# Rearranging the first part, the SSD steps and the output weights of a Hymba-style encoder step on one Trainium2 core

## The chip, the core and the metric

The kernel runs on one core of a Trainium2 chip. The metric is the device time of one execution in microseconds (us), as the median of several runs. Five engines work side by side and each takes its instructions strictly in its program's order: TensorE (PE in the profile, with PEld for its weight loads), VectorE (DVE), ScalarE (ACT), GpSimd (POOL) and SyncE (SP). DMAs are issued here from the instruction queues of SP and ACT, so an issue that must wait holds up whatever stands behind it on that engine.

## The reference

One layer of a streaming encoder is computed for 2048 prompt tokens and for 8 streams of 16 sample tokens; together they are 17 tiles of 128 tokens.

```
n = rmsnorm(x, norm1_g)
z, xbc, dt_raw, q, k, v, f_raw = split_columns(n @ w_in)
y_ssd = ssd_mixer(z, conv(xbc), dt_raw, ...)      # 8 heads, state 128, gate, group norm
y_fox = attention(q, k, v) with forget gates       # 8 heads of 64, causal
h = x + concat(y_ssd, y_fox) @ w_out
x = h + (silu(conv(n2 @ w_up)_g) * conv(n2 @ w_up)_v) @ w_down,   n2 = rmsnorm(h, norm2_g)
y = rmsnorm(x, final_norm_g)
```

The keys, values, forget logs, SSD states and convolution rows are outputs too. A matrix product with a weight matrix is made of three products of high and low parts ("hi" and "lo"): `split` rounds an fp32 tile to `hi` and subtracts to get `lo`.

## The kernel before

**Stages.** The prompt is cut into four parts of 512 tokens (two windows of 256 each; part 0 also carries the sample tile). `a_head(p)` makes the normalized, transposed input `nT` of a part: `sizes` finds each token's row size, a diagonal matrix `dg` of it is multiplied with ones into a PSUM tile (L203), and `rows` scales the transposed x with it (L208), then splits the product into hi (ACT, L102) and lo (POOL for the first half of the rows of a window, DVE for the second, L105). `a_body(p)` multiplies `nT` with the columns of `w_in`, 256 or 272 columns at a time with tokens as output rows (`proj_tm`, L366 to L368) or 128 columns at a time as output rows (`proj_cm`, L413 to L415). Each weight tile is loaded (`craw`) and split by ACT and POOL into `cmw`.

**Attention** runs over 4 x 8 (part, head) pairs and 320 units. A unit is one step of `t_phase`: a 128x512 score tile (L692, L693), its exponential on ACT (L697), and, two units behind, the product with the values (L662). One step of `s_phase` for the next head goes with it: a score tile (L634) whose maximum DVE takes (L637). `end` normalizes two heads: four reciprocals (L680) and a product.

**Filling.** TensorE's order is written out by hand in the loop at the end of the function. `fill` says how many credits of projection work (`part_steps`, later `out_steps`) go into a unit, and `sides` how many steps of `sample_attention` or of `ssd_chunk` are spread over a part's units. Before unit 0 the loop runs eight score steps with 1.5 credits of projection each. The word `"wait"` lets four units pass without filling. The other engines' orders come from a scheduler that looks at this order.

**SSD.** `ssd_chunk(c)` handles one tile of 128 tokens: loads, the decay matrix `sg` (a DMA broadcast, a subtraction on POOL L499, a minimum on DVE L500, an exponential on ACT L501), transposes, products, gate and norm. The sample tile `SMP` has eight inner steps, one for each stream: it loads that stream's state into `s0`, a buffer of the tag `yl` (two buffers, which attention uses too), multiplies (L555, L559), updates it on DVE (L561, L562) and stores it.

**Output.** When the projections are done, the pools of stage A are closed and `out_weights` loads and splits all eight tiles of `w_out` in one go (L853, L102, L105); three "wait" words follow, then `out_proj` runs as filling. After attention come the last output tiles and the feed-forward part (`ffn_part`), which fills the second half of the time.

**Tags.** A tile's tag names a ring of buffers: `cmw` 3, `xt` 2, `k12` 4 (attention's keys), `yl` 2, `sg` 1, `raw` 2. The profile's names drop the numbers, so `k12` is `k` and `q12` is `q`.

## Time and profile before

| what | us |
|---|---|
| median of 3 runs | 3183.7 (3178.56 to 3184.08) |
| the profiled execution's own time | 3180.02 |
| its span, first to last instruction | 3178.3 |
| TensorE busy | 3035.1 (95%) |
| VectorE busy | 1829.3 (58%) |
| ScalarE busy | 1024.1 (32%) |
| GpSimd busy | 882.4 (28%) |
| mean granted TensorE clock | 0.978 |

Busy time of an engine is the union of its instructions. PEclk is the share of full clock that TensorE was granted; a matmul at 0.50 takes twice its time and counts as busy. A row of a timeline has start, duration, engine, line, operation and tiles, and in brackets how long the engine had been idle and who ended that. A row of waits has the total, the number of waits and the longest. A row of grouped instructions has the count, then busy time and the mean in ns, then the idle time of the engine ahead of them and who ended it. An engine's name with a q is its instruction queue, which issues a DMA.

### The profile page before, as it was taken

To read this page: it belongs to the slowest core of one execution; us is meant where nothing else is said; L and a number is where in the kernel's file an instruction comes from. 1 tells how busy PE (TensorE), PEld (TensorE's weight loads), DVE (VectorE), ACT (ScalarE), POOL (GpSimd) and SP (SyncE) were. 2 spreads that over 40 slices of the span, in tenths; PEclk is the share of its full clock that TensorE was granted. 3 is DMA by queue.
4 is the path that set the end of the run, shared out by engine and by line. 5 is a ranking of instruction groups with operands and counts; after the bars stand their busy time and mean duration, and the time that the engine had idled before them with its cause. 6 is when DMAs were issued, how large, how long until landed. Compare 5 with 4: busy or idle time off the path is not lost.

```text
span 3178.3 us, 45508 instructions
## 1 busy us (share of the span) xinstructions
PE 3035.1 (95%) x17808; PEld 2671.8 (84%) x17808; DVE 1829.3 (58%) x3325; ACT 1024.1 (32%) x1778; POOL 882.4 (28%) x574
## 2 busy tenths in 40 slices
PE   5998988899999998999999999999999999999999
PEld 5886866788778875677899999989999999999998
DVE  5355465757574655552355555566555556766666
ACT  3343332434333433322322222233222223322222
POOL 3223311332232223100232232323232232433332
PEclk9998988999999998999999999999999999999999
DMA  4856864576547545543621221233122222322221
GB/s 161 256 180 197 246 200 128 165 215 178 148 152 211 157 137 178 169 144 111 234 79 58 64 67 54 67 100 100 53 74 60 67 66 71 109 74 80 68 71 67
DMA packets 233854, 398.36 MB, mean 125 GB/s; under 512 B 62624, under 2 KB 118568, under 8 KB 233640
## 3 DMA queue, kind: packets, MB, share of 16 engines
q1 hardware_dynamic: 180072, 234.22, 23.9%
q10 hardware_dynamic: 53568, 161.24, 16.2%
q8 instruction: 140, 2.29, 0.3%
q14 instruction: 74, 0.61, 0.1%
HBM read 317.13 MB, written 78.25 MB: 124 GB/s over the span
## 4 chain that ended last, share of the span: by engine, by line
PE 84%; DMA 7%; DVE 4%; issue 2%; SPq 1%; POOL 1%; ACT 1%; ACTq 0%; POOLq 0%; DVEq 0%
PE mm L113 11%; PE mm L114 11%; PE mm L115 11%; PE pv L662 6%; PE dn L975 5%; PE dn L976 5%; PE dn L977 5%; PE mm L413 3%; PE mm L414 3%; PE mm L415 3%; PE dn L873 2%; PE mm L366 2%; PE dn L875 2%; PE mm L367 2%; PE dn L874 2%; PE mm L368 2%
## 5 line engine op out<-in xcount | busy, mean ns | idle before, releaser
L105 POOL TENSOR_TENSOR wr<-raw,wr 128x1024 fp32r<-128x1024 f32 x198 | 475.9, 2411 | 1032.8 <-ACT wr L102 985.8
L113 PE MATMUL mm<-nT,wr 128*128 128x386 f32 (+1 forms) x2112 | 696.5, 330 | 1.3 <-ACT wr L102 0.8
L114 PE MATMUL mm<-nT,wr 128*128 128x386 f32 (+1 forms) x2112 | 695.3, 329 | 0.1
L115 PE MATMUL mm<-nT,wr 128*128 128x386 f32 (+1 forms) x2112 | 694.5, 329 | 0.0
L953 DVE SCALAR_TENSOR_TENSOR ac<-mm,cw,ac 128x384 f32<-128x384 f32 (+1 forms) x528 | 301.7, 572 | 345.0 <-ACT ac L951 337.3
L951 ACT ACTIVATE ac<-mm,cw 128x384 f32<-128x384 f32 (+1 forms) x264 | 172.5, 653 | 785.9 <-PE mm L115 782.0
L978 DVE TENSOR_TENSOR y<-y,dn 128x512 f32<-128x512 f32 x374 | 255.3, 684 | 267.3 <-PE dn L977 264.5
L114 PEld LDWEIGHTS mm<-nT,wr 128*128 128x128 f32 x2112 | 399.4, 189 | 6.8 <-DVE nT L105 0.3
L113 PEld LDWEIGHTS mm<-nT,wr 128*128 128x128 f32 x2112 | 397.6, 188 | 7.7 <-ACT wr L102 1.1
L115 PEld LDWEIGHTS mm<-nT,wr 128*128 128x128 f32 x2112 | 398.0, 188 | 5.7
L105 POOL TENSOR_TENSOR cmw<-craw,cmw 128x1024 fp32r<-128x1024 f32 (+1 forms) x96 | 231.1, 2411 | 380.4 <-ACT cmw L102 295.9
L413 PE MATMUL mm<-nT,cmw 128*128 128x256 f32 (+2 forms) x1024 | 309.2, 302 | 1.6 <-DVE g_2k L300 1.6
L637 DVE TENSOR_REDUCE nm<-s 128x1 f32<-128x512 f32 (+2 forms) x320 | 192.5, 606 | 190.2 <-PE s L634 109.4
L414 PE MATMUL mm<-nT,cmw 128*128 128x256 f32 (+2 forms) x1024 | 298.6, 292 | 0.0
L415 PE MATMUL mm<-nT,cmw 128*128 128x256 f32 (+2 forms) x1024 | 297.9, 291 | 0.0
L662 PE MATMUL pv<-pr,v 128*128 128x512 f32 (+3 forms) x640 | 295.6, 552 | 2.2 <-POOL v L602 1.8
L975 PE MATMUL dn<-wr,ht 128*128 128x512 f32 x748 | 294.4, 394 | 2.8 <-DVE y L978 1.7
L976 PE MATMUL dn<-wr,ht 128*128 128x512 f32 x748 | 292.8, 391 | 0.0
L977 PE MATMUL dn<-wr,ht 128*128 128x512 f32 x748 | 290.1, 391 | 0.0
L102 ACT CAST wr<-raw 128x1024 fp32r<-128x1024 f32 x198 | 203.2, 1042 | 173.7 <-PE dn L977 161.5
L697 ACT ACTIVATE pr<-s 128x512 f32<-128x512 f32 (+1 forms) x320 | 169.7, 531 | 269.7 <-PE s L693 182.9
L634 PE MATMUL s<-ks,q 68*128 68x512 f32 (+2 forms) x320 | 201.4, 635 | 10.8 <-DMA q<-q_d 7.0
(287 smaller groups left out, 5194.9 us busy)
## 6 DMA issues: line engine op xcount, KB each, us to landing
raw<-in_w_up ACTq DMA_DIRECT2D x132, 512.0 KB
raw<-in_w_down ACTq DMA_DIRECT2D x66, 512.0 KB
craw<-in_w_cm ACTq DMA_DIRECT2D x64, 512.0 KB
k<-k_d SPq DMA_DIRECT2D x80, 256.0 KB
craw<-in_w_tm ACTq DMA_DIRECT2D x24, 512.0 KB
q_d<-qk SPq DMA_DIRECT2D x96, 128.0 KB
k_d<-qk SPq DMA_DIRECT2D x96, 128.0 KB
ks<-k_d SPq DMA_DIRECT2D x80, 136.0 KB
```

The costliest lines, as they stand in the source:

```text
L105: leng.tensor_sub(lo, src, hi.bitcast(F32))
L113: T.matmul(ps[:, :W], whi(k), wt[:, 0, k, :W], start=k == 0, stop=False)
L114: T.matmul(ps[:, :W], whi(k), wt[:, 1, k, :W], start=False, stop=False)
L115: T.matmul(ps[:, :W], wlo(k), wt[:, 0, k, :W], start=False, stop=k == n - 1)
L413: T.matmul(ps[:, :W], wc[:, 0, k, :], wk[:, 0], start=k == 0, stop=False)
L414: T.matmul(ps[:, :W], wc[:, 0, k, :], wk[:, 1], start=False, stop=False)
L415: T.matmul(ps[:, :W], wc[:, 1, k, :], wk[:, 0], start=False, stop=k == KT - 1)
L662: m = T.matmul(pv[:, of:512], vr[:, jj], pr[:, :512 - of], start=first, stop=last)
L953: V.scalar_tensor_tensor(ac[:, 0:n], ps[:, j:j + n], cw2[:, ct, j:j + 1], ac[:, 0:n], op0=ALU.mult, op1=ALU.add)
L975: T.matmul(ps, ht[:, 0, ts_], wd[:, 0, cc], start=x == 0, stop=False)
L976: T.matmul(ps, ht[:, 0, ts_], wd[:, 1, cc], start=False, stop=False)
L977: T.matmul(ps, ht[:, 1, ts_], wd[:, 0, cc], start=False, stop=x == len(g) - 1)
```

## The change

**Part 0's head.** The row sizes no longer come from a second copy of x. `sizes_by_columns` squares the transposed tiles that are loaded anyway (ACT), and sums them by 8 matmuls with a column of ones per token tile (40 in all, L186 of the changed file). The diagonal is made on ACT instead of DVE (`diagonals`). The transposed x has its own tag `xT` of two buffers. The first window is prepared ahead of the first projection; the second and the sample tile are prepared between the first four half tiles of it. The twelve DMAs of constant rows (L1110 in the old file) are now issued at step 12 of the body.

**Heads of parts 1 to 3** are cut into more steps (sizes at step 12, diagonals at step 40, each window's rows in two halves), with waits of 1, 3 and 1 units instead of one of 4. `xt` has one buffer instead of two.

**SSD.** Two more steps for each chunk; chunk 3 moves from part 1 to part 2, and the counts in `sides` are set to the real number of steps. The subtraction and the minimum become eight `Relu` activations, one for each head, and the exponential takes the sign. `s0` takes its buffer from `k12`.

**Attention.** The four reciprocals and the closing product of `end` are queued as `chores`, one for each following unit. The eight first steps get 3.0 credits each.

**Weights.** `split2` makes lo on POOL in two halves; `proj_tm`, `proj_cm` and `out_weights` use it. `out_weights` loads two tiles ahead (on SP's queue instead of ACT's), splits one tile at a time behind the latest exponential, and waits 3 units first and 2 after each tile, so 19 units in place of 12.

```diff
+    def split2(src, hi, lo, leng):
+        S.copy(hi, src)
+        m = src.shape[1] // 2
+        for c in (slice(0, m), slice(m, 2 * m)):
+            leng.tensor_sub(lo[:, c], src[:, c], hi[:, c].bitcast(F32))
...
+        def sizes_by_columns(n, xTs):
+            sq = at([P, 2, 4, 256], "cmw", WA)
+            for kk in range(2):
+                S.activation(sq[:, kk, :, :n * P], xTs[kk][:, :, :n * P], AF.Square)
+            pz = tpt()
+            for c in range(n):
+                for k in range(KT):
+                    T.matmul(pz[:, c:c + 1], sq[:, k // 4, k % 4, c * P:(c + 1) * P], ones[:, 0:1], start=k == 0, stop=k == KT - 1)
+            ss = at([P, 2], "ss", 4)
+            V.tensor_scalar(ss[:, 0:n], pz[:, 0:n], 1.0 / D, EPS, op0=ALU.mult, op1=ALU.add)
+            G.tensor_tensor(ss[:, 0:n], ss[:, 0:n], mhalf[:, 0:n], op=ALU.pow)
...
-                dg = at([P, P], "dg", 4)
-                V.tensor_scalar_mul(dg, ident, ss)
+                dg = at([P, P], "dg", 2)
+                S.activation(dg, ident, AF.Identity, scale=x)
...
-        G.tensor_sub(sg, sg, acs[:, c].unsqueeze(2).to_broadcast([P, 8, P]))
-        V.tensor_scalar_min(sg, sg, 0.0)
-        S.activation(sg, sg, AF.Exp)
+        for h in range(8):
+            S.activation(sg[:, h], sg[:, h], AF.Relu, scale=-1.0, bias=acs[:, c, h:h + 1])
+        S.activation(sg, sg, AF.Exp, scale=-1.0)
...
-                s0 = bt_([P, 512], "yl", 2)
+                s0 = bt_([P, 512], "k12", KB)
...
-                    V.reciprocal(dn[:, cc], dn[:, cc])
+                    chores.append(lambda cc=slice(a * P, (a + 1) * P): V.reciprocal(dn[:, cc], dn[:, cc]))
+                chores.append(norm)
...
+        load(0)
+        load(1)
+        yield ("wait", 3)
         for k in range(KT):
-            raw = op.tile([P, D], F32, tag="raw", name="raw", bufs=2)
-            dW(raw, i["w_out"][0, k * P:(k + 1) * P, :])
             w = op.tile([P, 2, D], F32R, tag="wo", name="wo", bufs=KT)
-            split(raw, w[:, 0], w[:, 1], S, G)
+            with tc.issue_after(exps[-1]):
+                split2(raws[k], w[:, 0], w[:, 1], G)
             wo.append(w)
+            if k + 2 < KT:
+                load(k + 2)
+            yield ("wait", 2)
...
-    sides = {0: (sample_attention, 5 * NB + 1), 1: (lambda: chunks(SMP, 0, 1, 2, 3), 66), 2: (lambda: chunks(4, 5, 6, 7), 40),
-             3: (lambda: chunks(*range(8, 16)), 80)}
+    sides = {0: (sample_attention, 5 * NB + 1), 1: (lambda: chunks(SMP, 0, 1, 2), 49), 2: (lambda: chunks(3, 4, 5, 6, 7), 51),
+             3: (lambda: chunks(*range(8, 16)), 81)}
...
-                credit += 1.5
+                credit += 3.0
```

**What it moves.** First, ScalarE at the program's start. In the kernel before, five loads of x in its first layout (`in_xr`) stand ahead of the weights (`craw`), and the squares are of these:

```order
L98 DMA g1c<-in_g1c 128x8
L169 DMA cmw<-in_xr 128x1024 x5
L356 DMA craw<-in_w_tm 128x1088
L174 ACT_TABLE_LOAD
L174 ACTIVATE cmw,ss<-cmw 128x1024
L356 DMA craw<-in_w_tm 128x1088
L174 ACTIVATE cmw,ss<-cmw 128x1024 x3
```

In the kernel after, `xT` and `qk` are the transposed x of the first and second window:

```order
L98 DMA g1c<-in_g1c 128x8
L387 DMA craw<-in_w_tm 128x1088 x2
L182 ACT_TABLE_LOAD
L182 ACTIVATE cmw<-xT 128x1024 x2
L109 CAST cmw<-craw 128x1088 x2
L1123 ACTIVATE abc<-abc 128x8
L387 DMA craw<-in_w_tm 128x4x256
L182 ACTIVATE cmw<-qk 128x1024 x2
L387 DMA craw<-in_w_tm 128x4x256
L206 ACTIVATE dg<-ident,ss 128x128 x2
L102 CAST nT_134<-xT 128x4x256 x2
```

The `xr` loads are gone, and the diagonals and casts of the first window now stand behind the weights' casts and behind the squares of the second window.

Second, the decay matrix of an SSD chunk in part 2. In the kernel before, VectorE has the minimum (L500) among its maxima (L637):

```order
L533 TENSOR_TENSOR yt_8376<-yt_8376,s_8443 128x512
L467 SCALAR_TENSOR_TENSOR cth_8426<-cth_8426,cac_8425 128x256
L637 TENSOR_REDUCE nm_8333<-s_8488 128x1
L500 TENSOR_SCALAR sg_8813<-sg_8813 128x1024
L458 SCALAR_TENSOR_TENSOR cac_8503<-mm_8460,cw1_219,cac_8503 128x256
L637 TENSOR_REDUCE nm_8333<-s_8521 128x1
```

In the kernel after, ScalarE has the whole chain among its exponentials (`pr`) and evictions (`ev`):

```order
L733 ACTIVATE pr_9151<-s_9148 128x512
L419 ACTIVATE ev_9187<-mm_9135 128x256
L733 ACTIVATE pr_9195<-s_9192 128x512
L532 ACTIVATE sg_9396<-sg_9396,acs_185 128x128 x8
L533 ACTIVATE sg_9396<-sg_9396 128x1024
L109 CAST cmw_9469<-craw_9467 128x1088
L733 ACTIVATE pr_9233<-s_9230 128x512
```

The instruction that waits for the DMA of `sg` has moved from GpSimd to ScalarE, and nothing of the chain is left on VectorE.

Third, GpSimd at the output weights (`wo`). In the kernel before, with the memory fills of the value tiles (`v`) and the decay chain between them:

```order
L105 TENSOR_TENSOR wo_12535<-raw_12533,wo_12535 128x1024
L499 TENSOR_TENSOR sg_12763<-sg_12763,acs_235 128x1024
L105 TENSOR_TENSOR wo_12540<-raw_12538,wo_12540 128x1024
L602 MEMSET v_12855 128x4x64
L105 TENSOR_TENSOR wo_12545<-raw_12543,wo_12545 128x1024
L105 TENSOR_TENSOR wo_12550<-raw_12548,wo_12550 128x1024
L108 TENSOR_SCALAR ss_12736<-ss_12736 128x2
```

In the kernel after:

```order
L636 MEMSET v_12976 128x4x64
L112 TENSOR_TENSOR wo_12878<-raw_12734,wo_12878 128x512 x2
L557 TENSOR_TENSOR xe_12867<-xd_12863,te_186 128x512
L636 MEMSET v_13056 128x4x64
L112 TENSOR_TENSOR wo_12938<-raw_12826,wo_12938 128x512 x2
L636 MEMSET v_13143 128x4x64
L112 TENSOR_TENSOR wo_13001<-raw_12882,wo_13001 128x512 x2
```

Each pair of halves now has a fill or an SSD step between it and the next. Counted on TensorE's order by its L692 (L728 in the changed file), the units without any projection work ahead of the output products are 222 to 235 before and 224 to 251 after; around the head of part 1 they are 11 to 14 before and 9 to 15 after, around that of part 2 they are 51 to 54 before and 52 to 58 after.

More of the change, by code (lines that the diff above doesn't have):

```diff
@@ new lines, in a_head, with load @@
+                todo.append((e, w, SMP, 1, PAD1 + w[1] - w[0], i["xTs"]))
+        def load(e, w, c0, n, col, xsrc):
+            xTs = []
+            for kk in range(0, KT, 4):
+                xT = at([P, 4, 256], "qk" if first and e and n == 2 else "xT", 2)
+                dma(xT[:, :, :n * P], xsrc[:, kk:kk + 4])
+                xTs.append(xT)
+            return xTs
+        def sizes_by_columns(n, xTs):
[9 more added lines that the diff above has]
+            G.tensor_tensor(ss[:, 0:n], ss[:, 0:n], mhalf[:, 0:n], op=ALU.pow)
+            return [ss[:, c:c + 1] for c in range(n)]
@@ new lines, in sizes, with diagonals @@
+        def sizes(c):
+            ss = at([P, 2], "ss", 4)
+            for hf in range(2):
+                xt = at([P, 512], "xt", XB)
+                dA(xt, i["xr"][c][:, hf * 512:(hf + 1) * 512])
+                S.activation(xt, xt, AF.Square, accum_out=ss[:, hf:hf + 1])
+            V.tensor_add(ss[:, 0:1], ss[:, 0:1], ss[:, 1:2])
+            rsq(ss[:, 0:1], D)
+            return ss[:, 0:1]
+        def diagonals(ss):
+            dgs = []
+            for x in ss:
+                dg = at([P, P], "dg", 2)
+                S.activation(dg, ident, AF.Identity, scale=x)
@@ L211, in rows @@
                       V if kk else G)
-        ds = []
+                if not kk:
+                    yield
         if first:
             for t in todo:
-                rows(*t, sizes(*t))
-            yield 0.0
-            return
-        for t in todo:
-            ds.append(sizes(*t))
-        yield 0.0
-        for t, d in zip(todo, ds):
-            rows(*t, d)
-            yield 0.0
+                xTs = load(*t)
+                dgs = diagonals(sizes_by_columns(t[3], xTs))
+                yield
+                for _ in rows(*t, xTs, dgs):
+                    pass
+                yield
+            return
+        xTs = load(*todo[0])
+        ss = [sizes(todo[0][2] + c) for c in range(4)]
+        yield
+        dgs = diagonals(ss[0:2])
+        yield
+        yield from rows(*todo[0], xTs, dgs)
+        xTs = load(*todo[1])
+        dgs = diagonals(ss[2:4])
+        yield
+        yield from rows(*todo[1], xTs, dgs)
+        yield
     def gates(p, dtf):
@@ L357, in proj_tm @@
                 we = at([P, 2, 4, 272], "cmw", WA, F32R)
-                split(raw[:, :, :n], we[:, 0, :, :n], we[:, 1, :, :n], S, G)
+                split2(raw[:, :, :n], we[:, 0, :, :n], we[:, 1, :, :n], G)
                 wm.append(we)
@@ L402, in load_cm @@
             wc = at([P, 2, KT, P], "cmw", WA, F32R)
-            split(raw[:, 0:D].rearrange("p (k c) -> p k c", c=P), wc[:, 0], wc[:, 1], S, G)
+            split2(raw[:, 0:D].rearrange("p (k c) -> p k c", c=P), wc[:, 0], wc[:, 1], G)
             return wc
@@ L657, in hybrid_step @@
     pv_ins = []
-    late = []
+    late, chores, exps = [], [], []
     def weigh(pv, vr, jj, of, pr, first, last, end):
@@ L710, in t_rest @@
             weigh(a[0], *x)
+        while chores:
+            chores.pop(0)()
     def attention():
@@ L1035, in ffn_part @@
             finish(c)
-    for _ in a_head(0):
-        pass
+    head0 = a_head(0)
+    next(head0)
+    next(head0)
     tri = cb.tile([P, P], F32, name="tri")
@@ L1127, in part_steps @@
                 break
-            if k == 12 and hd:
+            if k in (12, 40) and hd:
                 next(hd)
@@ L1133, in part_steps @@
         next(hd)
-        yield "wait"
+        yield ("wait", 1)
         next(hd)
-        for c in hd:
-            pass
+        yield ("wait", 3)
+        next(hd)
+        yield ("wait", 1)
+        next(hd)
         bodies.append(a_body(p + 1))
@@ L1148, in out_steps @@
         open_out()
-        psum["wo"] = out_weights()
-        yield "wait"
-        yield "wait"
-        yield "wait"
+        yield from out_weights()
         for c in [SMP] + list(range(11)):
```

77 lines of the change are left out of this document (33 added, 44 removed).

## The prediction

> **What bounds the kernel now.** I read the page first, then the busy times in stretches, then the waits of TensorE. The page says that TensorE is the bound and that its clock is not always full:
>
> ```profile
> PE 3035.1 (95%) x17808; PEld 2671.8 (84%) x17808; DVE 1829.3 (58%) x3325; ACT 1024.1 (32%) x1778; POOL 882.4 (28%) x574
> PEclk9998988999999998999999999999999999999999
> ```
>
> So only what makes TensorE idle or slow can be gained. I cut the span at the places where the clock or the busy share falls (stretch, its length, then busy us and count for PE, PEld, DVE, ACT and POOL, then clock, DMA share and GB/s):
>
> ```profile
> 0.00:39.00 39.00, 3.51 (x9) 2.34 (x10) 24.04 (x59) 13.83 (x19) 18.08 (x31) 1.00 0.57 200
> 39.00:144.00 105.00, 103.00 (x734) 101.33 (x734) 37.23 (x106) 30.01 (x69) 31.79 (x14) 1.00 0.67 200
> 144.00:163.00 19.00, 14.20 (x70) 10.72 (x69) 12.22 (x42) 7.40 (x17) 4.62 (x7) 0.73 0.84 289
> 163.00:255.00 92.00, 88.11 (x689) 80.84 (x688) 49.66 (x144) 35.25 (x74) 24.07 (x16) 0.98 0.57 179
> 255.00:306.00 51.00, 40.27 (x304) 31.32 (x303) 29.23 (x72) 23.36 (x50) 17.03 (x15) 0.77 0.56 190
> 306.00:450.00 144.00, 136.93 (x1165) 118.13 (x1165) 77.98 (x198) 52.58 (x115) 39.96 (x22) 0.98 0.80 237
> 450.00:478.00 28.00, 18.51 (x125) 15.19 (x124) 17.09 (x30) 7.48 (x15) 5.24 (x3) 0.76 0.51 150
> 478.00:550.00 72.00, 57.05 (x302) 48.13 (x301) 35.94 (x71) 15.50 (x31) 12.47 (x9) 0.86 0.42 131
> 550.00:600.00 50.00, 42.41 (x275) 34.49 (x274) 37.39 (x69) 20.81 (x41) 16.67 (x15) 0.90 0.51 163
> 600.00:1190.00 590.00, 573.97 (x3826) 468.58 (x3825) 362.35 (x678) 234.35 (x464) 162.79 (x127) 0.99 0.58 170
> 1190.00:1240.00 50.00, 34.92 (x99) 21.43 (x99) 26.19 (x31) 18.70 (x29) 21.93 (x14) 0.69 0.64 195
> 1240.00:1577.00 337.00, 333.96 (x1567) 248.43 (x1565) 155.84 (x243) 98.08 (x189) 32.52 (x55) 1.00 0.49 161
> 1577.00:3178.00 1601.00, 1588.29 (x8666) 1490.89 (x8666) 964.14 (x1587) 466.80 (x668) 495.23 (x250) 1.00 0.24 73
> ```
>
> What a stretch loses is its length less (PE busy times clock). In order that gives 35.5, 2.0, 8.6, 5.7, 20.0, 9.8, 13.9, 22.9, 11.8, 21.8, 25.9, 3.0 and 12.7 us, together 193.6. The change doesn't touch the last two stretches; 178 us can be fought for, and no more.
>
> A short wait costs twice, as one place shows (a score tile that had waited, and the 4 us behind it):
>
> ```profile
> 697.95 0.47 PE L692 MATMUL s<-q,k 128*128 128x512 f32 x1 [2.12 <-DVE xd L565]
> 698.00:702.00 4.00, 4.00 (x12) 2.54 (x13) 2.96 (x6) 2.63 (x8) 0.80 (x2) 0.57 0.50 168
> ```
>
> A wait of 2.12 us was followed by a clock of 0.57 over 4 us, another 1.7 us. The Trainium skill (TensorE: Matmul & The Clock Gate, "HAM oscillation") says that only idle gaps above some 3.4 us should be avoided. The row disagrees, and I follow the row; what the sum would be by the rule is the fourth rival.
>
> **The start.** The first projection matmul is at 39.12:
>
> ```profile
> 1.21 7.04 ACTq L169 DMA_DIRECT2D cmw<-in_xr  x5
> 9.62 1.28 ACT L174 ACT_TABLE_LOAD   x1 [9.62 <-DMA cmw<-in_xr]
> 28.62 1.82 SPq L206 DMA_DIRECT2D qk<-in_xTw  x2
> 33.35 3.22 DVE L208 SCALAR_TENSOR_TENSOR qk<-qk,g1c,tp 128x256 f32<-128x256 f32 x8 [5.06 <-DMA qk<-in_xTw]
> 39.12 0.57 PE L366 MATMUL mm<-cmw,nT 128*128 128x272 f32 x1
> ```
>
> TensorE's order has all five diagonals ahead of it, the fifth needs the second window's `xTw`, and that load is issued at 28.62, behind the constant rows. In the new order only the first window stands ahead. The durations for its chain, by rows of like kind:
>
> ```profile
> L174 ACT ACTIVATE cmw<-cmw 128x1024 f32<-128x1024 f32 x5 | 5.2, 1050 | 0.9 <-DVE dg L184 0.8
> L203 PEld LDWEIGHTS tp<-dg,ones 128*128 128x128 f32 x34 | 6.3, 243 | 37.7 <-DVE dg L184 36.7 <-issue 0.9
> L105 POOL TENSOR_TENSOR cmw<-craw,cmw 128x1024 fp32r<-128x1024 f32 x88 | 210.3, 2393 | 349.8 <-ACT cmw L102 268.6 <-issue 40.3 <-DMA yl<-out_v 7.3
> ```
>
> I take 7 us for the landing of `xT` (no row shows it without the `xr` loads; bounds 4.6, the 28.62 to 33.35 above, and 9.62). Then table 1.3, two squares 2.1, two weight casts 2.1, and GpSimd has both weight splits (4.8) ahead of its power, so the diagonals come at about 17 to 18. Ones product 0.8, the first four scalings 1.6, cast 1.05, lo 2.4: the first projection runs at about 24. From there the 24 sums of the other two groups, at 0.24 to 0.5 each, and about 3 us of waiting for their diagonals come in between, so that of the 15 us only 9 remain (bounds 3 and 14). Should the 24 sums stall fully behind the second `xTw`, the 3 remain.
>
> **First attention units** (144 to 163, 8.6 lost): twice the projection between the eight first score steps (3.0 credits for 1.5) covers the chain from maximum to shift on which the first scores wait. I take 6 back, of 0 to 8.
>
> **The decay chain.**
>
> ```profile
> L499 POOL TENSOR_TENSOR sg<-sg,acs 128x1024 f32<-128x1024 f32 x17 | 32.3, 1903 | 105.2 <-DMA sg<-ac_d 56.9 <-PE s L540 16.1 <-DMA k<-k_d 15.3
> L500 DVE TENSOR_SCALAR sg<-sg 128x1024 f32<-128x1024 f32 x17 | 25.6, 1507 | 47.1 <-POOL sg L499 47.1
> L501 ACT ACTIVATE sg<-sg 128x1024 f32<-128x1024 f32 x17 | 18.0, 1058 | 69.5 <-DVE sg L500 69.5
> L697 ACT ACTIVATE pr<-s 128x128 f32<-128x128 f32 x32 | 8.8, 274 | 12.7 <-PE s L695 12.4 <-issue 0.2
> L184 DVE TENSOR_SCALAR dg<-ident,ss 128x128 f32<-128x128 f32 x17 | 16.7, 984 | 5.8 <-POOL ss L109 5.3 <-PE tp L203 0.5
> ```
>
> VectorE stands 47.1 us at L500 waiting for GpSimd, with the maxima behind it. At the worst place
>
> ```profile
> 797.07 0.47 SPq L498 DMA_DIRECT2D sg<-ac_d  x1
> 808.22 0.76 DVE L500 TENSOR_SCALAR sg<-sg 128x1024 f32<-128x1024 f32 x1 [7.14 <-POOL sg L499]
> ```
>
> it waits 7.14. The minimum takes 0.76 there and 1.51 in the mean; the small diagonal takes 0.98 in the mean, so both are often stretched while GpSimd works. The change takes both off VectorE. In place of 1.9 + 1.5 + 1.06 there are eight activations of 0.27, 2.2 us, and the same exponential, 17 x 2.2 = 37 us more on an engine that is 32% busy. The wait for the load now stands on ScalarE with exponentials and evictions behind it; but ScalarE waited 69.5 us there already, at L501, for the end of the longer chain. I put the new waits at 8 us for all 17 chunks (half a us each; 0 to 12 in the forecast, more in the third rival), and the gains where the chain lay: 8 of 13.9 in 450 to 478, where the decay of the sample chunk stands (bounds 3 and 13), and 11 of 21.8 in 600 to 1190 (bounds 4 and 19). The reciprocals, now one in a unit, and the two steps more for each chunk belong to the same gain: they take work out of bursts, and add none.
>
> **The sample chunk's states.**
>
> ```profile
> PE s L555 <- DMA yl<-in_s0T: 13.8, 4, 4.3
> ```
>
> Four waits, since a state is loaded only when the one two before it is stored. In 478 to 550 they and the slow clock behind them cost most of 22.9. In the four buffers of `k12` a state can be loaded three tiles ahead. Attention's keys then queue behind the states: twice the buffer of a key tile comes free only one unit ahead of its use. Such a unit has 24 projection matmuls (0.14 each by the second stretch, 3.4 us) beside its own work and the state's products, against 4.7 for a load (28.62 to 33.35 above), so little or nothing of it is bare. I take 18 back, of 12 to 22.
>
> **Heads of parts 1 and 2** (255 to 306, 20.0; 550 to 600, 11.8). Diagonals leave VectorE, scalings come in fours, and GpSimd's splits are halves. But the stretch without projections grows from 4 units to 7 in both. I take 6 and 4 back (bounds 0 to 14, and 0 to 9).
>
> **The output weights** (1190 to 1240, 25.9):
>
> ```profile
> L105 POOL TENSOR_TENSOR wo<-raw,wo 128x1024 fp32r<-128x1024 f32 x8 | 19.2, 2406 | 8.7 <-ACT wo L102 7.0 <-DMA v<-out_v 1.7
> 1204.16 3.06 DVE L500 TENSOR_SCALAR sg<-sg 128x1024 f32<-128x1024 f32 x1 [5.00 <-POOL sg L499]
> 1180.00:1190.00 10.00, 10.00 (x68) 6.22 (x67) 5.84 (x10) 4.21 (x7) 2.08 (x3) 1.00 0.71 245
> ```
>
> Eight splits, 19.2 us, crowd GpSimd; the decay chain and with it VectorE wait behind them. Ahead of them, from 1180 to 1190, the same units without projections keep TensorE busy for the whole 10 us at full clock. So 28 such units instead of 14 are no loss in themselves: their projections are done later at full rate, and attention alone fills TensorE when nothing crowds. With one split for every three units or so I take 17 back, of 9 to 23.
>
> **The sum.** 9 + 6 + 8 + 11 + 18 + 6 + 4 + 17 = 79 gained, 8 of new waits: 71. From the span of 3178.3 that is 3107, and 1.7 us lie around it (the profiled execution took 3180.0): 3109. The median of the runs shown, 3183.7, is 3.7 above that execution; I allow for a part of it: 3110. Costed at nothing: the 96 projection weights' `split2` (the same elements in two instructions, on an engine that is 28% busy), the constants behind the second window's load (their readers are attention's loads, and its units begin at 144), and the last chunk's end near unit 319 (its tile is the last to be multiplied, behind four others; bare, its norm would cost a few us). With every upper bound the gain is 122 (14 + 8 + 13 + 19 + 22 + 14 + 9 + 23), so 3058; with every lower one (3, 0, 3, 4, 12, 0, 0, 9) and 12 of new waits it is 19, so 3161.
>
> **Rivals.**
>
> *The waits change places.* TensorE still waits in the longer stretches without projections, behind keys that queue with the states, and behind the one-buffered `xt`:
>
> ```profile
> L179 ACT ACTIVATE xt<-xt 128x512 f32<-128x512 f32 x24 | 15.0, 628 | 29.4 <-DMA xt<-in_xr 18.9 <-DVE dg L184 4.7 <-DVE zs L835 4.7
> ```
>
> With one buffer each of these loads waits on SP's queue for the square before it, and keys, queries and values stand behind it there: at most the 15.0 us of the squares. For this rival: only 4 units have to be covered now, and 20.0 are lost there. Then half of what the heads, the states and the output weights give is gone (22 of 45), new waits double (16), and the 15 come on top: 79 - 22 - 16 - 15 = 26 gained, and 3178.3 + 1.7 - 26 is 3154.
>
> *Slower: ScalarE is held at the loads of `sg`.* The instruction that waits stands one unit or less behind the product that frees the buffer. A load as at 797.07 lasts until at most 808.2, some 9 us by then with GpSimd's 1.9 taken off; with 2.2 and 1.06 behind it an exponential is 12.5 late, of which two units of 3 us are covered. That leaves 6.5, and 1.7 for the clock: 8.2 for each of 17 chunks, 139 us, and 3178.3 - 79 + 139 gives 3240. It decides from 79 / 17 = 4.6 us each. Against it: ScalarE's 69.5 us of waiting at L501 today is 4.1 a chunk, mostly hidden. Were 6 us bare in the mean, the time would be 3203; ScalarE's casts of projection weights behind it would add to that.
>
> *No change*: TensorE's waits are set by landings (DMA share 0.80 and more around 150 and 400) that the change moves but doesn't speed up: 3180.
>
> *Short waits at full clock.* In 39 to 1240 the clock alone, (1 - PEclk) x busy, cost 51 us. If the remaining waits, each under 3 us, left it full, 15 more would be gained: 3095. This is what the Trainium skill's rule makes of it; the row at 697.95 speaks against it.
>
> **How the numbers follow.** Forecast 0.66, waits that change places 0.20, full clock 0.05, no change 0.04, slower 0.05. About 0.2%, 6 us, can be told from no change. Faster 0.66 + 0.20 + 0.05 = 0.91, same 0.04, slower 0.05. The range reaches from 3062, near the upper bounds, to 3163, which takes in most of the first rival; about 2 in 10 lie outside.
>
> **What would show it.** In the new trace the first projection should run at 20 to 28 us. No wait of L588 for `in_s0T` should be above 1 us, and no VectorE wait for GpSimd's `sg` exists. The stretch of the output weights should have a clock above 0.9. The mean clock, 0.978 now, should be above 0.985. The forecast is wrong if ScalarE's wait for `sg` is followed by idle TensorE of more than 2 us at most chunks, or if the units around the heads show the same clock of 0.77 and 0.90 over a longer stretch.

## The result, and the profile after

The changed kernel took 3159.1 us in the median (3158.1 to 3160.5, 4 executions) against 3181.1 for the kernel before beside it: a ratio of 0.9936, with an interval of 0.9922 to 0.995. Timed again later it took 3158.2 (3146.5 to 3164.0, 6 executions; ratio 0.9913, 0.9894 to 0.9933). (Ratios and intervals are those on record; they differ from the quotient of the two medians by up to 0.0007.) So it is 22 to 26 us faster. The forecast was 71.

The page of the changed kernel, TensorE's line and the clock's:

```profile
PE 3039.0 (96%) x17888; PEld 2682.1 (85%) x17888; DVE 1788.8 (57%) x3294; ACT 1066.7 (34%) x1927; POOL 865.8 (27%) x654
PEclk9998999899999999999999999999999999999999
```

The busy times in stretches, cut at the places like those of before:

```profile
0.00:29.00 29.00, 11.70 (x50) 10.91 (x50) 14.70 (x46) 10.28 (x12) 11.79 (x22) 1.00 0.57 183
29.00:140.00 111.00, 105.41 (x722) 102.72 (x721) 36.16 (x104) 33.19 (x73) 36.93 (x30) 0.98 0.58 172
140.00:165.00 25.00, 21.11 (x137) 20.03 (x137) 14.16 (x44) 10.10 (x23) 9.34 (x10) 1.00 0.83 259
165.00:250.00 85.00, 76.11 (x565) 69.46 (x565) 46.40 (x132) 33.45 (x71) 23.26 (x24) 0.96 0.50 161
250.00:310.00 60.00, 45.39 (x336) 31.01 (x335) 31.50 (x82) 21.12 (x49) 12.57 (x14) 0.74 0.71 221
310.00:440.00 130.00, 123.95 (x1047) 109.61 (x1045) 64.17 (x163) 47.19 (x105) 39.76 (x35) 0.97 0.73 219
440.00:545.00 105.00, 97.76 (x694) 82.96 (x694) 63.62 (x135) 41.34 (x88) 24.49 (x22) 0.97 0.57 175
545.00:700.00 155.00, 142.75 (x964) 119.70 (x964) 90.44 (x187) 65.01 (x145) 45.83 (x49) 0.94 0.67 205
700.00:1020.00 320.00, 313.30 (x2049) 254.16 (x2048) 194.34 (x365) 140.34 (x294) 87.27 (x92) 0.99 0.58 171
1020.00:1155.00 135.00, 131.45 (x878) 107.94 (x878) 83.44 (x161) 60.73 (x128) 29.80 (x34) 0.99 0.48 146
1155.00:1245.00 90.00, 72.09 (x353) 48.30 (x352) 47.38 (x77) 41.33 (x81) 26.41 (x30) 0.91 0.63 185
1245.00:1560.00 315.00, 313.88 (x1473) 238.57 (x1472) 138.48 (x216) 96.82 (x196) 27.03 (x48) 1.00 0.49 165
1560.00:3157.50 1597.50, 1584.13 (x8644) 1486.71 (x8642) 963.97 (x1587) 465.75 (x666) 491.31 (x248) 1.00 0.23 73
```

One cost hides in the busy column, the sums of the squares (TensorE's groups in the first 60 us: count, busy us, mean ns):

```profile
L186 PE MATMUL tp<-ones,cmw 128*128 128x1 f32 x80 | 15.8, 329 | 7.1 <-ACT cmw L182 7.1
```

The 40 sums are 80 records and keep TensorE busy for 15.8 us, work that the kernel before did not have; I count it as lost. The clock column hides a second cost: its 1.00 ahead of 40 us is not the pace at which TensorE ran.

```profile
28.92 6.82 PE L186 MATMUL tp<-ones,cmw 128*128 128x1 f32 x32
39.55 0.43 PE L398 MATMUL mm<-cmw,nT 128*128 128x272 f32 x1
39.77 0.43 PE L399 MATMUL mm<-cmw,nT 128*128 128x272 f32 x1
41.38 1.84 PE L186 MATMUL tp<-ones,cmw 128*128 128x1 f32 x16
43.29 0.29 PE L398 MATMUL mm<-cmw,nT 128*128 128x272 f32 x1
43.41 0.29 PE L399 MATMUL mm<-cmw,nT 128*128 128x272 f32 x1
```

Equal matmuls follow each other every 0.22 us at 39.55 and every 0.12 us at 43.29, and 32 records of the sums take 6.82 us where 16 later ones take 1.84. The pace nearly doubles at 40.5 us here and at 43.1 in the kernel before; the trace has no clock record ahead of these times. The loss of each place (length less busy times clock), before and after:

| place | before | after | forecast gain | gain |
|---|---|---|---|---|
| start and first projections | 37.5 | 25.0 + 15.8 of sums | 9 | -3.3 |
| first attention units | 8.6 | 3.9 | 6 | 4.7 |
| units up to the head of part 1 | 5.7 | 11.9 | 0 | -6.2 |
| head of part 1 | 20.0 | 26.4 | 6 | -6.4 |
| rest of part 0's attention | 9.8 | 9.8 | 0 | 0 |
| sample chunk and its states | 36.8 | 10.2 | 8 + 18 | 26.6 |
| head of part 2, other chunks | 33.6 | 35.5 | 4 + 11 | -1.9 |
| output weights | 25.9 | 24.4 | 17 | 1.5 |
| rest | 15.7 | 14.5 | 0 | 1.2 |

That is 16 us; the spans differ by 20.8, and the clock's two digits, with the slow start that it does not show, are good for the difference. One row, the sample chunk's, holds more than the whole gain.

What waits now, by the waits of TensorE and of ScalarE:

```profile
PE s L570 <- ACT pr L733: 12.6, 2, 9.1
PE s L668 <- ACT pr L733: 11.2, 6, 5.1
PE mm L444 <- DVE cac L489: 8.6, 3, 5.0
PE s L588 <- DVE ss L198: 7.8, 1, 7.8
ACT xt L197 <- DMA xt<-in_xr: 64.7, 21, 6.3
ACT sg L532 <- DMA sg<-ac_d: 35.0, 14, 5.7
ACT wo L109 <- DMA raw<-in_w_out: 13.7, 3, 6.4
```

No wait for `in_s0T` is left. The two largest groups of TensorE's waits end at an exponential (`pr`) on ScalarE, and ScalarE itself stood at a load. Three of its rows show that, and one of TensorE's behind the last:

```profile
1033.81 2.15 ACT L532 ACTIVATE sg<-sg,acs 128x128 f32<-128x128 f32 x7 [5.71 <-DMA sg<-ac_d]
1180.42 1.04 ACT L109 CAST wo<-raw 128x1024 fp32r<-128x1024 f32 x1 [5.79 <-DMA raw<-in_w_out]
1230.82 1.04 ACT L109 CAST wo<-raw 128x1024 fp32r<-128x1024 f32 x1 [6.43 <-DMA raw<-in_w_out]
1238.16 2.08 PE L570 MATMUL s<-sst,xb 128*128 128x256 f32 x4 [9.06 <-ACT pr L733]
```

One of the large waits is VectorE's. Its rows ahead of 557 us, and the product that waits:

```profile
549.34 0.67 DVE L594 TENSOR_TENSOR k<-k,decs 128x512 f32<-128x512 f32 x1
550.21 3.09 DVE L229 SCALAR_TENSOR_TENSOR xT<-xT,g1c,tp 128x256 f32<-128x256 f32 x8
553.22 2.55 DVE L717 TENSOR_TENSOR yl<-yl,rdb 128x512 f32<-128x512 f32 x1
556.89 0.18 DVE L582 COPY cm<-xb 128x32 f32<-128x32 f32 x1
557.13 1.22 PE L588 MATMUL s<-k,cm 128*128 128x256 f32 x2 [7.85 <-DVE ss L198]
```

The page names `ss`, but VectorE was simply busy: both halves' scalings came in one row of eight, then `norm` (L717), and `cm`, which the product needs, stood behind them and two short rows.

### The profile page after: what moved, and what is told of

The parts are those of the page before. It is cut to its first block, busy times and chain, and to the rows that moved or that the text cites. A ratio compares the mean times of both kernels' runs of the same rounds, so it can differ in the third digit from the quotient of the medians.

```text
span 3157.5 us, 45849 instructions
## 1 busy us (share of the span) xinstructions
PE 3039.0 (96%) x17888; PEld 2682.1 (85%) x17888; DVE 1788.8 (57%) x3294; ACT 1066.7 (34%) x1927; POOL 865.8 (27%) x654
## 3 DMA queue, kind: packets, MB, share of 16 engines
q10 hardware_dynamic: 51696, 154.43, 15.8%
## 4 chain that ended last, share of the span: by engine, by line
PE 85%; DMA 8%; DVE 2%; ACT 2%; issue 1%; SPq 1%; POOL 1%; ACTq 0%; DVEq 0%; POOLq 0%
PE mm L120 11%; PE mm L121 11%; PE mm L122 11%; PE pv L696 6%; PE dn L1025 5%; PE dn L1026 5%; PE dn L1027 5%; PE mm L444 3%; PE mm L445 3%; PE mm L446 3%; DMA xt<-in_xr 2%; PE dn L923 2%; PE dn L925 2%; PE dn L924 2%; PE mm L397 2%; PE mm L399 2%
## 5 line engine op out<-in xcount | busy, mean ns | idle before, releaser
L112 POOL TENSOR_TENSOR cmw<-craw,cmw 128x512 fp32r<-128x512 f32 (+1 forms) x192 | 248.6, 1317 | 467.8 <-ACT cmw L109 348.1
```

## The experiments

All runs are compared with the kernel before; "on after" is the difference of medians from 3158.6, the middle of the two above. Single executions of one kernel lay up to 18 us apart, so a difference of 5 us is not told from none.

**The states alone.** The kernel before with one line changed.

```diff
-                s0 = bt_([P, 512], "yl", 2)
+                s0 = bt_([P, 512], "k12", KB)
```

> The kernel before with one line of the change: the sample states take their buffer from the keys' four instead of the two of yl. Theory (the sample chunk is the one term of the sum that came as forecast, and what else the change gains it loses again elsewhere): 15 to 25 us faster than before, ratio 0.992 to 0.995, as fast as the whole change, and no wait of the states' product for in_s0T above 1 us. Rival (the gain between 450 and 550 us comes from the Relu chain, the longer chunk steps and chunk 3's move as much as from the buffers): 5 to 10 us, ratio 0.997 to 0.998.

3157.6 us, ratio 0.9925 (0.9912 to 0.9939). No wait for `in_s0T`. This one line brings as much as the whole change; everything else in it comes, in sum, to about nothing.

**Sizes without the sums.**

```diff
-                dgs = diagonals(sizes_by_columns(t[3], xTs))
+                dgs = diagonals(sizes_by_rows(t[2], t[3]))
```

with the loads and squares of `xr` as before, into `cmw`.

> The kernel after, but part 0's row sizes come from the rows of x again (one load of 512 KB for each token tile, a square with a running sum on ScalarE), in the new order with only the first window ahead of the first projection; the 40 sums on TensorE go. Theory (the sums take 15.4 us of TensorE time at full clock, which is what the earlier start gave): the first projection stays at 22 to 28 us and the time falls by 8 to 16 us, ratio to after 0.995 to 0.9975. Rival (the sums lie in time in which TensorE would wait for loads anyway, and the five loads of x push the weights back): within 4 us of after, or slower by up to 8.

3146.0 us, 0.9893 (0.9877 to 0.9909), 13 on after, first projection at 23.3. Counted on TensorE's order, the 51st projection matmul starts at 47.3 us in the kernel before and at 47.3 in after, and here at 39.5; the 201st at 66.4, 67.4 and 60.0. So the 15 us by which after begins its projections earlier were gone after 50 of them, and without the sums 6 to 8 us of the earlier start are kept. With the rows loaded into `k12` and `q12`, and all but the first window's on SyncE's queue:

> The kernel after with part 0's sizes from rows of x again, as in the run that took the 40 sums away, but the rows are loaded into attention's idle buffers (k and q), the first window's from ScalarE's queue and the others' from SyncE's, so that no load stands in front of ScalarE's casts of nT (8.1 us there). Theory (sums and a held ScalarE were all that kept the start from its gain): first projection at 17 to 20 us instead of 23.3, 4 to 8 us faster than that run, 15 to 22 us faster than after, ratio to before 0.986 to 0.989. Rival (the second window's rows and transposes come later on SyncE's queue, behind the constant rows, and the wait moves there): within 3 us of that run.

3143.8 us, 0.9881 (0.9865 to 0.9896): no more than the run before. ScalarE still stood ahead of its casts:

```profile
21.66 0.39 ACTq L396 DMA_DIRECT2D craw<-in_w_tm  x1
22.09 1.99 ACT L102 CAST nT<-xT 128x1024 fp32r<-128x1024 f32 x2 [8.07 <-DMA q_d<-q]
```

The third weight load, an issue on ScalarE, waited until a constant row that SyncE had issued (`q_d<-q`) was written: the issue stands behind a wait on a semaphore that this DMA counts up too, whose last count came at 21.57. So the rows were moved as well (`v_st` lists the stores of `v`):

```diff
-                constant_rows()
+                with tc.issue_after(v_st[-1]):
+                    constant_rows()
```

> The run with the sizes from rows in attention's buffers, and the twelve DMAs of the constant rows issued behind the last store of v of the first projection's window, on SyncE's queue. Theory (ScalarE stood 8 us at the third weight load, which waits for the end of a constant row's DMA, with the casts of nT behind it): first projection at 17 to 20 us instead of 23.2, no ScalarE wait above 3 us between 13 and 22 us, 3 to 7 us faster than without the edit: 3136 to 3141 us, ratio to before 0.985 to 0.987. Rival (the weight load waits for GpSimd's splits anyway, to 17.6, or the second window's rows are late next): within 2 us.

3147.5 us, 0.9886 (0.987 to 0.9902). The first projection did come earlier, and the time did not:

```profile
15.15 0.39 ACTq L397 DMA_DIRECT2D craw<-in_w_tm  x1
15.72 1.05 ACT L102 CAST nT<-xT 128x1024 fp32r<-128x1024 f32 x1 [1.61 <-DVE xT L239]
16.82 0.59 PE L407 MATMUL mm<-cmw,nT 128*128 128x272 f32 x1 [2.83 <-ACT nT L102]
57.66 3.78 SPq L1172 DMA_DIRECT2D k_d<-q  x4
61.53 3.08 SPq L421 DMA_DIRECT2D out_v<-ev  x3
65.77 0.37 ACT L420 COPY ev<-mm 128x256 f32<-128x256 f32 x1 [8.24 <-DMA out_v<-ev]
```

The cause named was right (8.07 to 1.61, first projection at 16.8); now the stores of `v` queue behind the constant rows and the evictions wait for their buffers. The 201st projection matmul is 4.6 us earlier than without the edit (53.0 against 57.6), the 301st 2.3 later (74.1 against 71.8).

**Loads of the heads' rows four steps ahead of their squares.**

```diff
                 dA(xt, i["xr"][c][:, hf * 512:(hf + 1) * 512])
+                yield
                 S.activation(xt, xt, AF.Square, accum_out=ss[:, hf:hf + 1])
...
-            if k in (12, 40) and hd:
+            if (k % 4 == 0 and 4 <= k <= 36 or k == 40) and hd:
```

> The kernel after, but each half row of x for the heads of parts 1 to 3 is loaded four projection steps ahead of its square, one half at a time, instead of all eight at step 12; still one buffer, same number of units without projections. Theory (ScalarE and SyncE stand in order at the loads of the one xt buffer; the units without projections only show it): ScalarE's wait of 64.7 us for in_xr falls below 15, the loss of the stretches 165 to 250, 250 to 310 and 545 to 580 us falls from 52.7 by 15 to 30 in all, the time by as much, ratio to after 0.990 to 0.995. Rival (it is the longer stretch without projections that lays every wait bare): the wait for in_xr goes, others take its place, and the time falls by less than 5 us.

3160.5 us, 0.9929 (0.9912 to 0.9947), no gain. ScalarE's wait hardly fell:

```profile
ACT xt L198 <- DMA xt<-in_xr: 58.2, 19, 5.8
```

Nothing on TensorE stands before these loads, so the scheduler issues them soon after the one buffer is free, whatever the step (the first thirteen from 108 to 192 us in after, from 107 to 196 us here). The edit did not do what it says, so the one buffer is not tested by it. For the wait of 7.85 us at 557, the rows of VectorE above show another cause.

**Output weights into seven buffers.** Tiles three ahead into `raw`, `y` and the halves of `mx`, same 28 units:

```diff
+            if 3 <= k < 7:
+                if k % 2:
+                    raws["m"] = op.tile([P, 2, D], F32, tag="mx", name="mx", bufs=2)
+                raws[k] = raws["m"][:, 1 - k % 2]
...
-            if k + 2 < KT:
-                load(k + 2)
+            if k + 3 < KT:
+                load(k + 3)
```

> The kernel after, but the output weights' tiles are loaded three ahead into seven buffers (those of raw, y and mx, which are empty then), so that no load waits for a buffer and no cast for a load just issued; the 19 units of waiting are kept. Theory (ScalarE stands in order at a load of w_out just issued, 5.8 and 6.4 us, with exponentials behind it): the waits of TensorE of 5.1 and 9.1 us at 1177 and 1229 us are gone or below 2, the time falls by 8 to 16 us, ratio to after 0.995 to 0.9975. Rival (28 units without projections lay bare whatever is late next, the sg loads and the values): within 4 us of after.

3160.3 us, 0.9936 (0.9921 to 0.995). Its stretches:

```profile
1155.00:1245.00 90.00, 81.61 (x406) 57.09 (x405) 50.64 (x86) 43.99 (x90) 27.04 (x32) 0.96 0.63 197
1245.00:1560.00 315.00, 307.38 (x1433) 233.47 (x1432) 135.78 (x209) 97.34 (x194) 28.95 (x47) 0.98 0.49 166
1548.84 0.69 PE L120 MATMUL mm<-nT,wr 128*128 128x386 f32 x1 [5.62 <-ACT wr L102]
```

The loss at the weights fell from 24.4 to 11.7 and that of the next stretch rose from 1.1 to 13.8, 10.7 us of that between 1540 and 1560: the feed-forward part's first weights now had to be waited for, their loads being held on ScalarE's queue until 1546.8. The wait of 5 us at the first cast stayed. Waits of 5 and 1 units in place of 3 and 2 on top:

> The kernel after with the seven buffers for the output weights, and in addition five units instead of three ahead of the first cast and one instead of two after each tile: 22 units without projections instead of 28. Theory (the first cast waits because its load is issued three short units earlier, about 9 us): no TensorE wait above 2 us between 1155 and 1245 us; 8 to 16 us faster than after, unless the feed-forward part's first weights again wait for buffers near 1545 us (7.4 us there with seven buffers alone), then 2 to 8 us. Rival (the casts and splits come in a denser row and GpSimd holds VectorE as in the kernel before): within 4 us of after or slower, clock below 0.85 there.

3160.8 us, 0.9928 (0.9914 to 0.9942). The wait at the first cast went (no wait above 2.1 us there), and the 5.62 at the feed-forward part came again. Gain given back later, twice.

**The old decay chain, and a later Relu.**

```diff
-        for h in range(8):
-            S.activation(sg[:, h], sg[:, h], AF.Relu, scale=-1.0, bias=acs[:, c, h:h + 1])
-        S.activation(sg, sg, AF.Exp, scale=-1.0)
+        G.tensor_sub(sg, sg, acs[:, c].unsqueeze(2).to_broadcast([P, 8, P]))
+        V.tensor_scalar_min(sg, sg, 0.0)
+        S.activation(sg, sg, AF.Exp)
```

> The kernel after with the decay chain of before: subtraction on GpSimd, minimum on VectorE, exponential on ScalarE, in place of the eight Relu. Theory (the move shortens the chain, but what ScalarE waits at the loads of sg eats most of that): 0 to 8 us slower than after. Rival 1 (the move is worth its 19 us of the prediction, hidden in the total by losses elsewhere): 14 to 22 us slower, with VectorE waits for GpSimd of 5 us and more followed by idle TensorE. Rival 2 (ScalarE held at sg costs more than the old chain): 3 to 12 us faster, and TensorE's waits at 471 (5.0), 1032 (3.6) and 1200 us (2.1) are gone.

3164.0 us, 0.9937 (0.9923 to 0.9952): 5 slower than after, just what can be told. VectorE's wait for GpSimd is back (46.8 us, 14 times, longest 6.9), and GpSimd now waits for the loads of `sg` (124.5 us, 14 times) where ScalarE waited 35.0. The other edit puts the three new lines behind the score products of the next step:

> The kernel after, but the eight Relu and the exponential of a chunk stand one step later in the chunk, behind the score products instead of right behind the load of sg; nothing else moves. Theory (ScalarE stands in order at a load just issued): ScalarE's wait for sg, 35.0 us, falls below 20, TensorE's waits at 471, 1032 and 1200 us, 10.6 in all, fall by half or more, the time by 5 to 12 us. Rival (the scheduler puts the Relu where it stood, since nothing else is ready, or the exponentials that wait there are covered): within 3 us of after. If the decay then comes too late for the product with xd, up to 8 us slower.

3156.2 us, 0.9915 (0.9901 to 0.9928): within the spread. ScalarE's wait for `sg` did not fall (39.3 us, 15 times): probably one step is less than a load takes.

**Credits.** 1.5 for 3.0 in the first steps.

> The kernel after with 1.5 credits of projection instead of 3.0 for each of the eight score steps ahead of unit 0. Theory (the 5.5 us gained between 140 and 165 us come from these credits): 3 to 7 us slower than after, a clock below 0.85 between 140 and 165 us. Rival (what was gained there comes from the order of the start and of the constant rows): within 3 us of after.

3159.5 us, 0.9927 (0.9912 to 0.9942). Between 140 and 165 us the loss went to 10.0 (17.40 busy at 0.86), so the gain there is due to the credits; the total did not follow.

**The heads.** First the second window's rows between the first half tiles of the next projections:

```diff
-        next(hd)
-        yield ("wait", 1)
-        next(hd)
         bodies.append(a_body(p + 1))
-        for c in bodies[p + 1]:
+        for k, c in enumerate(bodies[p + 1]):
             if c is None:
                 return
+            if k < 3:
+                next(hd, None)
```

> The kernel after, but in the heads of parts 1 to 3 the second window's rows are prepared between the first three half tiles of the next projections, as part 0's are, so that 5 units or so go without projections instead of 7. Theory (in the units without projections VectorE's row of eight scalings, normalizations and state updates is laid bare; it is neither the loads nor ScalarE): TensorE's waits of 7.9 us at 549, and of 2.9 and 3.2 us at 266 and 270, fall by half in all, the loss of the stretches 250 to 310 and 545 to 580 us, 40.9, falls by 10 to 25, ratio to after 0.992 to 0.997. Rival (the work of a window on VectorE has to be waited for wherever it stands; the projections come to wait instead): within 4 us of after.

3156.3 us, 0.9916 (0.9903 to 0.993): not told from after; the wait near 549 was now 10.8. Then the waits of 1, 3 and 1 units themselves, as 4 in one piece:

> The kernel after, but the heads of parts 1 to 3 leave four units in one piece without projections, between the first window's rows and the second's, as many as before, instead of 1, 3 and 1 with units between. Theory (what is bare in these stretches is VectorE's scalings, state updates and normalizations in a row, and it is bare for four units as for seven): the loss of 250 to 310 and 545 to 580 us, 40.9, changes by less than 8, the time stays within 5 us of after. Rival (the stretch was made longer, and each unit without projections costs 2 to 3 us): 8 to 16 us faster, with 20 and 12 us lost as in the kernel before.

3149.6 us, 0.9897 (0.9881 to 0.9913), 9 on after, so the rival seemed to hold. Its profiled execution was the slowest of six, and shows no place for the gain. So the reverse, 2, 4 and 2 units, with the changed kernel beside it:

> The kernel after with longer waits in the heads of parts 1 to 3: 2, 4 and 2 units instead of 1, 3 and 1, so three more units without projections in each head, nine in all. Theory 1 (the longer stretch itself cost the change 10 to 12 us, since each unit without projections loses 1 to 1.5 us): 6 to 16 us slower than after. Theory 2 (VectorE's row of work is bare once, whatever the length): within 4 us of after, and the gain of the run with four units comes from the place of the second window's rows, not from the number of units.

> The changed kernel itself once more, so that the small edits of this and the other runs have their base on one chip and the spread of single executions is seen. Expected: 3155 to 3163 us, ratio to before 0.992 to 0.995, single executions within 8 us.

3139.0 us, 0.9859 (0.9841 to 0.9876), beside 3158.2: 19 faster with more units, where both theories had the same or slower. Then 3, 5 and 3:

> The kernel after with still longer waits in the heads of parts 1 to 3: 3, 5 and 3 units instead of 1, 3 and 1, six more units without projections in each head. Theory 1 (longer stretches are better, since the heads' chains run behind attention units and the projections come later at full rate): not slower than the run with 2, 4 and 2, so 3128 to 3141 us. Theory 2 (it is the place that counts: which rows of VectorE, ScalarE and the queues meet at a unit, so that fewer and more units both helped by chance of position): anywhere between that run and after, 3143 to 3160 us, with a wait of 4 us or more at other units than in either.

3175.7 us, 0.9977 (0.9965 to 0.9989): 17 slower than after. Fewer, more and still more units give -9, -20 and +17, so the total does not follow the number. Where it goes shows when each run is cut at its own units without projections, counted on TensorE's order; cuts at fixed times would mislead, since the output weights begin at 1167 us in after and at 1223 with 3, 5, 3. What each stretch loses, in us, with the units of the stretches that have no projections:

| stretch | before | after, two profiles | 4 in one piece | 2, 4, 2 | 3, 5, 3 |
|---|---|---|---|---|---|
| head of part 1 | 15.0 (4 units) | 22.4, 20.7 (7) | 12.2 (4) | 27.2 (10) | 37.7 (13) |
| behind it | 54.2 | 22.4, 26.8 | 30.9 | 19.2 | 23.3 |
| head of part 2 | 9.7 (5) | 14.7, 17.3 (8) | 14.9 (5) | 9.3 (11) | 18.1 (14) |
| behind it | 13.0 | 6.6, 10.0 | 13.0 | 8.2 | 13.7 |
| head of part 3 | 8.4 (5) | 5.1, 6.3 (8) | 0.5 (5) | 0.3 (11) | 11.8 (14) |
| behind it | 1.1 | 7.8, 7.6 | 9.0 | 2.5 | 1.6 |
| output weights | 21.3 (14) | 24.1, 22.7 (28) | 11.6 (28) | 10.8 (28) | 11.7 (28) |
| behind, to the last unit | 7.5 | 0.3, 0.7 | 9.8 | 4.0 | 6.5 |

The rows of the head of part 1 and of the output weights, of after, of 2, 4, 2 and of 3, 5, 3:

```profile
261.47:301.89 40.42, 26.54 (x189) 15.73 (x187) 25.69 (x63) 18.24 (x42) 11.49 (x12) 0.68 0.65 206
1167.14:1241.38 74.24, 56.33 (x269) 36.37 (x268) 37.91 (x58) 34.63 (x68) 25.21 (x27) 0.89 0.68 199
260.24:313.44 53.20, 37.09 (x237) 21.30 (x235) 32.36 (x82) 22.28 (x52) 11.82 (x13) 0.70 0.68 214
1169.77:1233.83 64.06, 56.03 (x271) 35.41 (x269) 36.99 (x61) 34.17 (x69) 24.82 (x28) 0.95 0.66 209
257.39:328.59 71.20, 48.58 (x321) 28.07 (x319) 39.66 (x102) 25.47 (x60) 12.55 (x16) 0.69 0.68 215
1222.79:1285.47 62.68, 53.70 (x259) 34.69 (x258) 37.63 (x58) 29.00 (x54) 25.80 (x27) 0.95 0.70 211
```

The head of part 1 does follow the number: about 3 us for each unit in all four versions of the changed kernel. Most of that is moved, not added: with the stretch behind it the loss is 43 to 48 us for 4, 7 and 10 units, and 61 for 13. The later stretches do not follow the number. The output weights, which none of these edits touches, lose 24.1 and 22.7 in after and 10.8 to 11.7 in the other three. In after TensorE's largest waits there are 5.07 and 9.06 us; with 2, 4, 2 they are 4.03 and 2.15. Their loss goes with the unit at which they begin. In the seven kernels here that begin them at unit 224, and leave them as they are, they lose 22.3 to 24.1 us in every profile; in the four that begin at 221 they lose 11.4 to 11.6, with 9.3 to 9.8 behind them; in the two at 233, 10.1 and 10.8, with 2.5 and 4.0 behind. So a shift of some units in the heads changes which rows meet hundreds of us later, and does so alike each time.

**Together.** Rows in `k12`, second window between the half tiles, later Relu:

> Three edits together: part 0's sizes from rows in attention's buffers, the second window's rows between the first half tiles of the next projections, and the Relu one step later. If their gains on after (the first 15 to 22 us by theory, the other two 6 and 7 us as measured, partly the same waits) add: 3128 to 3138 us, ratio to before 0.983 to 0.986. If the two small ones were chance: as the first alone, 3137 to 3146.

3143.7 us, 0.9869 (0.9853 to 0.9886): as the first alone; the two small gains do not show on top of it. The start with late constant rows, and four units in one piece:

> The start of the run before this one and four units without projections in one piece in the heads of parts 1 to 3. If the 9 to 12 us of the four units are real and have nothing to do with the start, 8 to 12 us faster than with the start alone: 3125 to 3133 us, ratio to before 0.982 to 0.984. If they were the chance of six executions: within 4 us of the start alone.

3146.8 us, 0.9881 (0.9863 to 0.9898): 1 us on the start alone. The 9 us of the four units did not come again. Rows in `k12`, and 2, 4, 2:

> Waits of 2, 4 and 2 units and part 0's sizes from rows in attention's buffers, together. The first brought 19 us on after, the second 14 to 15, in different stretches. If they add: 3121 to 3129 us, ratio to before 0.980 to 0.983. If the start, which moves all later units by 10 us but not against each other, upsets the places: 3130 to 3142.

3129.0 us (3123.1 to 3130.9), 0.983 (0.9813 to 0.9846): 30 on after, 15 of it from the waits on this base, and it beats both kernels. The waits help in the same places as on after: the output weights and the stretch behind them lose 12.6 us (23.0 with the rows alone), the head of part 2 10.3 (15.7) and that of part 3 0.3 (6.2).

## Why the prediction went wrong, step by step

- **Sample chunk and states (8 + 18): right.** 26.6 by the traces, and the state line alone gives 24 us; cut by units, the stretch between the heads of parts 1 and 2 falls with that line from 54.2 to 32.4. The keys that queue with the states cost nothing that shows.
- **First attention units (6): right in its row**, 4.7, by the credits; but the next row is 6.2 worse, and the total keeps nothing of it that can be told.
- **Start (9): wrong.** The first projection came at 24.06, as worked out. The step that failed is "of the 15 us only 9 remain", and it does not follow from the prediction's own terms: 24 sums at 0.24 to 0.5 us are 5.8 to 12, and with 3 of waiting 0 to 6.2 remain. Measured, the 24 sums behind the first projection took 8.7 us (6.82 and 1.84) and the waits of 1.61 and 1.92 us came to 3.5; the rest went to the diagonals that now stand behind it and to the slow pace, for which the sum had no term: TensorE came to full pace only 2.6 us earlier than before (40.5 against 43.1). Nothing of the 15 us was left by the 51st projection matmul. The runs without sums get 13 to 15 back.
- **Decay chain (8 + 11, less 8 of new waits: 11 net): mis-sized.** Put back, the old chain costs 5 us in all, just what can be told. It shows where the sample chunk stands (31.8 lost between the heads of parts 1 and 2, against 22.4 and 26.8); the gain of 11 behind it shows in no stretch. ScalarE took over the waiting (35.0 us in 14 waits) where VectorE had 47.1.
- **Heads (6 and 4): wrong in sign.** The step that failed is the price of the longer stretch: the prediction says that it grows from 4 units to 7 and still takes 6 back. The head of part 1 loses about 3 us for each such unit, 22.4 where the kernel before lost 15.0; that of part 2 loses 14.7 where it was 9.7. In part 1 much of this comes back in the stretch behind the head (both together lose 44.8 and 47.5, and 48.3 in the kernel before with the state line), so 6 and 4 were not gained, and little was lost for good. That diagonals left VectorE was true and beside the point. In part 2 what lies bare is VectorE's row of eight scalings and whatever joins it (7.85 at 557).
- **Output weights (17): wrong.** I had costed the crowd on GpSimd, and it went. But ScalarE waits for the loads as before (13.7 us in 3 waits, 13.3 in 7 before): the first cast stood three short units behind its load, the load took some 9 us, and the exponentials stood behind the cast, so that TensorE stood 5.07 and 9.06. Curing that (11.7 lost, from 24.4) did not shorten the run, since the next stage's weights were then late. That rival, "the waits change places", forecast 26 gained and 3154, near to what came, though not through `xt`: no wait of that kind was shown bare.
- **ScalarE held at `sg`** decided from 4.6 us a chunk. The waits are 2.5 us each (35.0 / 14) and mostly covered; only some, as at 1033.81, are bare.
- **Short waits at full clock: no.** Behind a wait of 1.92 us at 44.8 the clock is 0.59 for 3.4 us:

```profile
46.75 0.49 PE L225 MATMUL tp<-dg,ones 128*128 128x128 f32 x2 [1.92 <-ACT dg L206]
46.80:50.20 3.40, 3.40 (x17) 3.40 (x18) 2.24 (x9) 1.25 (x2) 3.01 (x3) 0.59 0.15 17
```

  So the bound of some 3.4 us for idle gaps in the Trainium skill (TensorE: Matmul & The Clock Gate, "HAM oscillation") does not hold here either.
- **The mean clock** is 0.984, not above 0.985; the output weights have 0.91, as asked, at an unchanged loss: a clock says little when the engine is idle.

The common fault is in the sum. I valued a step by the wait that it takes away, as if the time behind it stayed as it is. The three runs with other waits show the same code, shifted by some units, 20 us better or 17 worse. The wide range did hold 3159, near its slow end; adding gains of 4 to 17 us did not give the time. What stays open is why unit 233 is a better place for the output weights than 224: the rows show where less is lost, not a rule by which to find such numbers.

## What to carry to other kernels

Before an operation is moved to another engine, ask what it waits for there, and what stands behind it in that engine's order: here a cast that waited 6 us for its load held the exponentials, and TensorE stood 9. That such a wait costs more on ScalarE than elsewhere is not shown: with the decay chain back on GpSimd and VectorE the kernel was 5 us slower. Work that fills an idle engine is not free if it pushes all that follows; price it by its own row and set it against the idle time that it replaces, and read the pace from equal rows where the clock column has no record. And test a change that moves many things part by part: one line can hold the whole gain, and a few units' shift can be worth more than the parts.

## What the runs showed of the hardware

A matmul with one moving column is not free. The records of the sums, 128x1 each, take 0.115 us at full pace (1.84 / 16) and 0.21 at the slow pace of the start (6.82 / 32), with weight loads of 188 to 333 ns beside them. The Trainium skill (TensorE: Matmul & The Clock Gate, "LDWEIGHTS (loading the stationary operand)") says that a load's time goes with its columns, P / 1.2 ns, so 107 for 128; the records at full pace agree to about a tenth, those at the slow pace take twice that. So the weights probably set the cost; no run here varies the columns to show it.

TensorE starts at little more than half pace, and the clock column does not say so: equal projection matmuls follow each other every 0.22 us up to 40.5 us in after, and every 0.12 behind that. The first projection stands 16 us ahead of the change in after, 4 in the kernel before, and 7 in the run without the sums (23.3 and 30.2). Why it took longest in after was not tested.

An issue on one engine can wait for a DMA of another's through a semaphore that both use: ScalarE stood 8.07 us until a constant row issued by SyncE was written, and 1.61 us, at another producer, when those rows were issued later.
